# Softmax cross-entropy over a 32000-word vocabulary: label gathers spread into the load stream, narrower last chunks, results written in four parts

## Chip, cores, metric

The kernel runs on one core of one Trainium2 chip. The metric is device time in microseconds (us) of one execution. Executions agree closely (2544.47 to 2544.96 us over 12 runs of the kernel before). The TensorE does no work here.

Engine names in the profile: DVE is the vector engine, ACT the scalar engine, POOL is GpSimd, SP is the sync engine. "Lnnn" is a line of the kernel that the view belongs to, so the same statement has another number before and after the change. "half" is the tile of the first DVE instruction on a chunk, which folds the chunk in half. The start of that instruction is taken as the moment at which a chunk has landed, where DVE was waiting for it; the landing is recorded 0.02 us earlier.

## The reference

```python
batch, seq, vocab = 16, 512, 32000          # logits f32 ~ N(0,1), labels int
logits_max  = np.max(logits, axis=-1, keepdims=True)
log_sum_exp = np.log(np.sum(np.exp(logits - logits_max), axis=-1)) + logits_max.squeeze(-1)
loss = log_sum_exp - logits[b, s, labels[b, s]]        # (16, 512) f32, rewritten
```

The logits are 8192 rows of 32000 floats, 1.049 GB, each read once. The output is 32 KB.

## The kernel before

128 partitions hold 64 rows each (JT = 64). A row comes in two chunks of 16000. POOL issues each load, which converts f32 to bf16 on the way. DVE takes the maximum (folding the chunk in half, then reducing), and ACT computes exp with the sum as a by-product. The logit at the label is fetched by 64 indirect loads, each bringing one block of 16 floats per partition.

```python
    W = 16000; NCH = 2                                    # cut
    data = ctx.enter_context(tc.tile_pool(name="data", bufs=4))
    scratch = ctx.enter_context(tc.tile_pool(name="scratch", bufs=3))
    nc.gpsimd.dma_start(out=labels_sb, in_=labels_pj)
    # ... index arithmetic on DVE -> ugather
    for j in range(JT):
        nc.gpsimd.indirect_dma_start(out=B_all[:, j], out_offset=None, in_=logits_blk,
            in_offset=bass.IndirectOffsetOnAxis(ap=ugather[:, j : j + 1], axis=0))
    # ... mask16 = (k16 == label & 15) * B_all ; G = sum over 16   (all rows at once)
    for j in range(JT):
        for c in range(NCH):
            chunk = data.tile([P, W], BF16)
            nc.gpsimd.dma_start(out=chunk, in_=logits_pjv[:, j, c * W : (c + 1) * W])
            half = scratch.tile([P, W // 2], BF16)
            nc.vector.tensor_tensor(out=half, in0=chunk[:, : W // 2], in1=chunk[:, W // 2 :], op=max)
            nc.vector.tensor_reduce(out=negm[:, c : c + 1], in_=half, axis=X, op=max, negate=True)
            nc.scalar.activation(out=chunk, in_=chunk, func=Exp, bias=negm[:, c : c + 1],
                                 scale=1.0, accum_out=ssum[:, c : c + 1])
        # ... weights exp(max_c - max) join the chunks: negM_all[:, j], S_all[:, j]
    nc.scalar.activation(out=lse, in_=S_all, func=Ln)
    # ... loss = lse - negM_all - G
    nc.gpsimd.dma_start(out=out_pj, in_=loss)
```

## Time and profile before

| | us |
|---|---|
| time, median of 12 runs | 2544.6 |
| span in the profiled run | 2542.9 |
| first chunk issued / first vector instruction on it | 84.7 / 106.5 |
| pace of the load stream, per chunk of 16000 | 18.89 |
| last chunk landed | 2505.2 |
| output issued / span ends | 2534.4 / 2542.9 |

From the page of the kernel before: its busy times, two of the rows of 40 equal slices of the span (busy tenths of the DMA engines, and GB/s written), and groups of instructions (line, engine, operation, out<-in, count; busy us, mean ns of one; idle time before them and its main releaser).

```profile
span 2542.9 us, 1282 instructions
DVE 1667.2 (66%) x456; ACT 1771.0 (70%) x323; POOL 131.7 (5%) x200
DMA  0799999999999999999999999999999999999993
GB/s 7 145 213 216 218 217 217 218 217 217 217 217 217 217 217 217 217 217 217 216 215 215 216 217 217 217 218 217 218 217 217 217 217 217 217 217 217 217 217 75
...
L139 ACT ACTIVATE chunk<-chunk,negm 128x16000 bf16<-128x16000 bf16 x128 | 1744.4, 13628 | 656.0 <-issue 629.1
L132 DVE TENSOR_REDUCE negm<-half 128x1 f32<-128x8000 bf16 x128 | 1086.2, 8486 | 4.2
L126 DVE TENSOR_TENSOR half<-chunk 128x8000 bf16<-128x8000 bf16 x128 | 553.7, 4325 | 759.4 <-DMA chunk<-in_logits_dram 759.4
L84 POOL DMA_INDIRECT B_all<-in_logits_dram,ugather x64 | 61.2, 957 | 20.0 <-issue 18.9
```

No compute engine is above 70%, while the DMA row stands at 9 in every slice but the first two and the last. DVE waits 759 us for chunks and needs 12.8 us (4.33 + 8.49) per chunk, ACT 13.8; a chunk arrives every 18.89 us. The load stream is the limit. 8.192 MB of f32 in 18.89 us is 434 GB/s. The Trainium skill, "DMA: Bandwidth & Descriptors", section Bandwidth, puts the ceiling of the fabric at 435 GB/s, and what this trace reads stands at that figure. The page derives it from the SBUF ports, however, and after the conversion to bf16 only 217 GB/s are written there, so which part sets the pace is not shown. The three weak slices are what there is to win.

From the timeline of the kernel before, its head and its end (start us, duration us, engine, line, what; idle before and releaser in brackets):

```profile
4.29 1.75 POOL L84 DMA_INDIRECT B_all<-in_logits_dram,ugather  x1 [0.83 <-DVE ugather L77]
6.34 0.96 POOL L84 DMA_INDIRECT B_all<-in_logits_dram,ugather  x1 [0.30 <-issue]
...
83.77 0.94 POOL L84 DMA_INDIRECT B_all<-in_logits_dram,ugather  x1 [0.30 <-issue]
84.70 2.27 POOL L122 DMA_DIRECT2D chunk<-in_logits_dram  x4
106.48 4.32 DVE L126 TENSOR_TENSOR half<-chunk 128x8000 bf16<-128x8000 bf16 x1 [17.90 <-DMA chunk<-in_logits_dram]
...
2505.18 4.32 DVE L126 TENSOR_TENSOR half<-chunk 128x8000 bf16<-128x8000 bf16 x1 [6.04 <-DMA chunk<-in_logits_dram]
2509.54 8.49 DVE L132 TENSOR_REDUCE negm<-half 128x1 f32<-128x8000 bf16 x1
2518.11 13.63 ACT L139 ACTIVATE chunk<-chunk,negm 128x16000 bf16<-128x16000 bf16 x1 [5.16 <-issue]
2532.04 1.28 ACT L178 ACT_TABLE_LOAD   x1
2534.40 0.55 POOL L186 DMA_DIRECT2D out_dram<-loss  x1 [77.23 <-DVE loss L185]
```

Until 84.7 us POOL issues gathers, one each 1.25 us, and the first chunk is issued right behind the last of them. At the end, the last chunk still has a full chain of DVE and ACT ahead of it, 28.9 us, and after the output is issued another 8.55 us pass.

### The profile page before, as it was taken

What the parts mean: (1) busy time and instruction counts of PE and PEld (TensorE: products, weight loads), DVE (VectorE), ACT (ScalarE), POOL (GpSimd) and SP (SyncE); (2) the same over time, 40 slices, a digit from 0 to 9 for tenths busy, and PEclk for the clock granted to TensorE, in tenths of its full rate; (3) what the DMA queues carried; (4) which work ended last, traced back from release to release, by engine and by line L of the source; (5) the groups of instructions that cost most, each with busy time, mean ns of one, the idle gap of its engine ahead of it and who ended that gap; (6) DMA issues with size and microseconds to landing.
All of it is one profiled execution on the core that took longest, in us unless ns stands there. A gap on an engine that the chain in (4) does not pass through costs nothing.

```text
span 2542.9 us, 1282 instructions
## 1 busy us (share of the span) xinstructions
DVE 1667.2 (66%) x456; ACT 1771.0 (70%) x323; POOL 131.7 (5%) x200
## 2 busy tenths in 40 slices
DVE  0276676676776766767767667667677676676674
ACT  0176777767767777777677677777776776777766
POOL 7200000000000000000000000000000000000000
DMA  0799999999999999999999999999999999999993
GB/s 7 145 213 216 218 217 217 218 217 217 217 217 217 217 217 217 217 217 217 216 215 215 216 217 217 217 218 217 218 217 217 217 217 217 217 217 217 217 217 75
DMA packets 20555, 525.01 MB, mean 206 GB/s; under 512 B 3104, under 2 KB 4128, under 8 KB 4160
## 3 DMA queue, kind: packets, MB, share of 16 engines
q0 software_dynamic: 20544, 524.92, 96.0%
q14 instruction: 11, 0.09, 0.0%
HBM read 1049.17 MB, written 0.03 MB: 413 GB/s over the span
## 4 chain that ended last, share of the span: by engine, by line
issue 94%; POOL 5%; DMA 0%; POOLq 0%; DVE 0%; PEldq 0%
POOL chunk L122 3%; POOL B_all L84 2%; DMA B_all<-in_logits_dram,ugather 0%; DMA labels_sb<-in_labels_dram 0%; POOLq L122 0%; POOLq L212 0%; DVE ugather L77 0%; DVE lab_hi L52 0%; DVE lab_lo L60 0%; PEldq L212 0%; POOLq L186 0%
## 5 line engine op out<-in xcount | busy, mean ns | idle before, releaser
L139 ACT ACTIVATE chunk<-chunk,negm 128x16000 bf16<-128x16000 bf16 x128 | 1744.4, 13628 | 656.0 <-issue 629.1
L132 DVE TENSOR_REDUCE negm<-half 128x1 f32<-128x8000 bf16 x128 | 1086.2, 8486 | 4.2
L126 DVE TENSOR_TENSOR half<-chunk 128x8000 bf16<-128x8000 bf16 x128 | 553.7, 4325 | 759.4 <-DMA chunk<-in_logits_dram 759.4
L122 POOL DMA_DIRECT2D chunk<-in_logits_dram x128 | 67.7, 530 | 2304.8 <-ACT chunk L139 1149.4
L139 ACT ACT_TABLE_LOAD x1 | 1.3, 1283 | 106.5 <-DMA chunk<-in_logits_dram 106.5
L84 POOL DMA_INDIRECT B_all<-in_logits_dram,ugather x64 | 61.2, 957 | 20.0 <-issue 18.9
L102 DVE TENSOR_TENSOR mask<-mask,B_all 128x1024 f32<-128x1024 f32 x1 | 1.2, 1226 | 81.0 <-DMA B_all<-in_logits_dram,ugather 81.0
L139 ACT ACTIVATION_READ_ACCUMULATOR chunk<-chunk,negm 128x1 f32 x128 | 23.8, 186 | 0.0
L164 DVE TENSOR_TENSOR sw<-ssum,wgt 128x2 f32<-128x2 f32 x64 | 9.7, 151 | 13.6 <-ACT wgt L156 13.6
L156 ACT ACTIVATE wgt<-negm,negM_all 128x2 f32<-128x2 f32 x64 | 17.9, 279 | 0.0
L167 DVE TENSOR_REDUCE S_all<-sw 128x1 f32<-128x2 f32 x64 | 9.9, 154 | 2.0
L149 DVE TENSOR_REDUCE negM_all<-negm 128x1 f32<-128x2 f32 x64 | 9.9, 154 | 2.0
L186 POOL DMA_DIRECT2D out_dram<-loss x1 | 0.6, 552 | 77.2 <-DVE loss L185 77.2
L52 DVE TENSOR_SCALAR lab_hi<-labels_sb 128x64 int32<-128x64 int32 x1 | 0.2, 195 | 3.4 <-DMA labels_sb<-in_labels_dram 3.4
L178 ACT ACT_TABLE_LOAD x1 | 1.3, 1283 | 0.0
L106 DVE TENSOR_REDUCE G<-mask 128x64 f32<-128x1024 f32 x1 | 1.2, 1220 | 0.0
L94 DVE TENSOR_TENSOR mask<-k,lab_lo 128x1024 f32<-128x1024 int32 x1 | 1.2, 1219 | 0.0
L92 POOL IOTA k<- 128x1024 int32 x1 | 1.2, 1217 | 0.0
L182 DVE TENSOR_TENSOR loss<-lse,negM_all 128x64 f32<-128x64 f32 x1 | 0.2, 224 | 1.2 <-ACT lse L178 1.2
L45 POOL DMA_DIRECT2D labels_sb<-in_labels_dram x1 | 0.7, 707 | 0.8 <-PEq L212 0.8
L178 ACT ACTIVATE lse<-S_all 128x64 f32<-128x64 f32 x1 | 0.3, 256 | 0.0
L77 DVE CUSTOM_DVE_ANT_0 ugather<-ublock,lab_hi 128x128 uint16<-128x128 uint16 x1 | 0.2, 225 | 0.0
(7 smaller groups left out, 1.0 us busy)
## 6 DMA issues: line engine op xcount, KB each, us to landing
chunk<-in_logits_dram POOLq DMA_DIRECT2D x128, 4000.0 KB
B_all<-in_logits_dram,ugather POOLq DMA_INDIRECT x64
labels_sb<-in_labels_dram POOLq DMA_DIRECT2D x1, 64.0 KB
out_dram<-loss POOLq DMA_DIRECT2D x1, 32.0 KB
```

The costliest lines, as they stand in the source:

```text
L84: nc.gpsimd.indirect_dma_start(out=B_all[:, j], out_offset=None, in_=logits_blk, in_offset=bass.IndirectOffsetOnAxis(ap=ugather[:, j : j + ...
L92: nc.gpsimd.iota(k16, pattern=[[0, JT], [1, 16]], base=0, channel_multiplier=0)
L94: nc.vector.tensor_tensor(out=mask16, in0=k16, in1=lab_lo4.rearrange("p (j one) -> p j one", one=1).to_broadcast([P, JT, 16]), op=mybir.Al ...
L122: nc.gpsimd.dma_start(out=chunk, in_=logits_pjv[:, j, c * W : (c + 1) * W])
L126: nc.vector.tensor_tensor(out=half, in0=chunk[:, : W // 2], in1=chunk[:, W // 2 :], op=mybir.AluOpType.max,)
L132: nc.vector.tensor_reduce(out=negm[:, c : c + 1], in_=half, axis=mybir.AxisListType.X, op=mybir.AluOpType.max, negate=True,)
L139: nc.scalar.activation(out=chunk, in_=chunk, func=mybir.ActivationFunctionType.Exp, bias=negm[:, c : c + 1], scale=1.0, accum_out=ssum[:, ...
L149: nc.vector.tensor_reduce(out=negM_all[:, j : j + 1], in_=negm, axis=mybir.AxisListType.X, op=mybir.AluOpType.min,)
L156: nc.scalar.activation(out=wgt, in_=negm, func=mybir.ActivationFunctionType.Exp, bias=negM_all[:, j : j + 1], scale=-1.0,)
L164: nc.vector.tensor_tensor(out=sw, in0=ssum, in1=wgt, op=mybir.AluOpType.mult)
L167: nc.vector.tensor_reduce(out=S_all[:, j : j + 1], in_=sw, axis=mybir.AxisListType.X, op=mybir.AluOpType.add,)
L178: nc.scalar.activation(out=lse, in_=S_all, func=mybir.ActivationFunctionType.Ln, bias=0.0, scale=1.0)
```

## The change

The intent is to start the stream at once, to keep it full, and to shorten what follows it. The gathers are placed after each row's chunks; labels and outputs go through SP; the last three rows are cut into narrower chunks; a fifth data buffer is paid for, in part, with one scratch buffer of half its size; the final arithmetic is done in four groups of 16 rows.

```diff
-    data = ctx.enter_context(tc.tile_pool(name="data", bufs=4))
-    scratch = ctx.enter_context(tc.tile_pool(name="scratch", bufs=3))
+    data = ctx.enter_context(tc.tile_pool(name="data", bufs=5))
+    scratch = ctx.enter_context(tc.tile_pool(name="scratch", bufs=2))
-    nc.gpsimd.dma_start(out=labels_sb, in_=labels_pj)
+    nc.sync.dma_start(out=labels_sb, in_=labels_pj)
-    for j in range(JT):
+    def issue_gather(j):
         nc.gpsimd.indirect_dma_start(out=B_all[:, j], ...)
-    k16 = persist.tile([P, JT, 16], INT32)
+    k16 = persist.tile([P, JT, 16], INT16)
+    edges = [0, 16, 32, 48, 64]; NQ = 3                  # shortened
+    def finale(jlo, jhi):      # mask, G, Ln, loss of these rows, then:
+        nc.sync.dma_start(out=out_pj[:, sl], in_=loss[:, sl])
     for j in range(JT):
+        widths = {-3: [8000] * 4, -2: [8000] * 2 + [4000] * 4,
+                  -1: [4000] * 6 + [2000] * 4}.get(j - JT, [W] * NCH)
         # ... the loop over chunks, now over widths
+        if j < last_g:                                   # last_g = 59
+            issue_gather(j)
+        elif j == last_g:
+            for jj in range(last_g, JT): issue_gather(jj)
         # ... joining of chunks
+        if (j + 1) in edges[1:]: finale(lo, j + 1)
-    nc.scalar.activation(out=lse, in_=S_all, func=Ln)    # and the rest, once for all rows
-    nc.gpsimd.dma_start(out=out_pj, in_=loss)
```

(Cut: renamed slices, an assertion, the branch for a row in one chunk, the iota of k16 that moves behind row 3.)

More of the change, by code (lines that the diff above doesn't have):

```diff
@@ L11 @@
 INT32 = mybir.dt.int32
+INT16 = mybir.dt.int16
 @with_exitstack
@@ L31 @@
     NCH = V // W
+    NCH_MAX = 16
     logits_2d = logits.rearrange("b s v -> (b s) v")
@@ L89 @@
         )
-    k16 = persist.tile([P, JT, 16], INT32)
-    nc.gpsimd.iota(k16, pattern=[[0, JT], [1, 16]], base=0, channel_multiplier=0)
+    k16 = persist.tile([P, JT, 16], INT16)
     mask16 = persist.tile([P, JT, 16], FP32)
-    nc.vector.tensor_tensor(
-        out=mask16,
-        in0=k16,
-        in1=lab_lo4.rearrange("p (j one) -> p j one", one=1).to_broadcast(
-            [P, JT, 16]
-        ),
-        op=mybir.AluOpType.is_equal,
-    )
-    nc.vector.tensor_tensor(
-        out=mask16, in0=mask16, in1=B_all, op=mybir.AluOpType.mult
-    )
@@ L105 @@
-    G = persist.tile([P, JT], FP32)
-    nc.vector.tensor_reduce(
-        out=G,
-        in_=mask16,
-        axis=mybir.AxisListType.X,
-        op=mybir.AluOpType.add,
-    )
+    G = persist.tile([P, JT], FP32)
     negM_all = persist.tile([P, JT], FP32)
     S_all = persist.tile([P, JT], FP32)
-    for j in range(JT):
-        negm = stats.tile([P, NCH], FP32)
-        ssum = stats.tile([P, NCH], FP32)
-        for c in range(NCH):
-            chunk = data.tile([P, W], BF16)
+    lse = persist.tile([P, JT], FP32)
@@ new lines @@
+    loss = persist.tile([P, JT], FP32)
+    if JT % 16 == 0 and JT >= 32:
+        edges = list(range(0, JT, 16)) + [JT]
+    else:
+        edges = [0, JT]
+    NQ = 3
+    def finale(jlo, jhi):
+        sl = slice(jlo, jhi)
+        nc.vector.tensor_tensor(
+            out=mask16[:, sl],
+            in0=k16[:, sl],
+            in1=lab_lo4[:, sl]
+            .rearrange("p (j one) -> p j one", one=1)
+            .to_broadcast([P, jhi - jlo, 16]),
+            op=mybir.AluOpType.is_equal,
+        )
+        nc.vector.tensor_tensor(
+            out=mask16[:, sl], in0=mask16[:, sl], in1=B_all[:, sl],
+            op=mybir.AluOpType.mult,
+        )
+        nc.vector.tensor_reduce(
+            out=G[:, sl],
+            in_=mask16[:, sl],
+            axis=mybir.AxisListType.X,
+            op=mybir.AluOpType.add,
+        )
+        nc.scalar.activation(
+            out=lse[:, sl],
+            in_=S_all[:, sl],
+            func=mybir.ActivationFunctionType.Ln,
+            bias=0.0,
+            scale=1.0,
+        )
+        nc.vector.tensor_tensor(
+            out=loss[:, sl], in0=lse[:, sl], in1=negM_all[:, sl],
+            op=mybir.AluOpType.subtract,
+        )
+        nc.vector.tensor_tensor(
+            out=loss[:, sl], in0=loss[:, sl], in1=G[:, sl],
+            op=mybir.AluOpType.subtract,
+        )
+        nc.sync.dma_start(out=out_pj[:, sl], in_=loss[:, sl])
@@ new lines @@
+    for j in range(JT):
+        small = j >= JT - NQ and W % 4 == 0 and JT > NQ
+        widths = {-3: [8000] * 4, -2: [8000] * 2 + [4000] * 4, -1: [4000] * 6 + [2000] * 4}.get(j - JT, [W] * NCH) if small else [W] * NCH
+        nchj = len(widths)
+        assert sum(widths) == V
+        starts = [sum(widths[:c]) for c in range(nchj)]
+        negm = stats.tile([P, NCH_MAX], FP32)
+        ssum = stats.tile([P, NCH_MAX], FP32)
+        for c in range(nchj):
+            wj, c0 = widths[c], starts[c]
+            chunk_t = data.tile([P, W], BF16, name="chunk")
+            chunk = chunk_t[:, :wj]
@@ L122 @@
             nc.gpsimd.dma_start(
-                out=chunk, in_=logits_pjv[:, j, c * W : (c + 1) * W]
+                out=chunk, in_=logits_pjv[:, j, c0 : c0 + wj]
             )
-            half = scratch.tile([P, W // 2], BF16)
+            half_t = scratch.tile([P, W // 2], BF16, name="half")
+            half = half_t[:, : wj // 2]
             nc.vector.tensor_tensor(
                 out=half,
-                in0=chunk[:, : W // 2],
-                in1=chunk[:, W // 2 :],
+                in0=chunk[:, : wj // 2],
+                in1=chunk[:, wj // 2 :],
@@ L146 @@
             )
-        if NCH > 1:
+        if j == 3:
+            nc.gpsimd.iota(k16, pattern=[[0, JT], [1, 16]], base=0, channel_multiplier=0)
+        last_g = max(0, JT - 5)
+        if j < last_g:
+            issue_gather(j)
+        elif j == last_g:
+            for jj in range(last_g, JT):
+                issue_gather(jj)
+        if nchj > 1:
             nc.vector.tensor_reduce(
                 out=negM_all[:, j : j + 1],
-                in_=negm,
+                in_=negm[:, :nchj],
                 axis=mybir.AxisListType.X,
@@ L154 @@
             )
-            wgt = stats.tile([P, NCH], FP32)
+            wgt = stats.tile([P, NCH_MAX], FP32)
             nc.scalar.activation(
-                out=wgt,
-                in_=negm,
+                out=wgt[:, :nchj],
+                in_=negm[:, :nchj],
                 func=mybir.ActivationFunctionType.Exp,
@@ L162 @@
             )
-            sw = stats.tile([P, NCH], FP32)
+            sw = stats.tile([P, NCH_MAX], FP32)
             nc.vector.tensor_tensor(
-                out=sw, in0=ssum, in1=wgt, op=mybir.AluOpType.mult
+                out=sw[:, :nchj],
+                in0=ssum[:, :nchj],
+                in1=wgt[:, :nchj],
+                op=mybir.AluOpType.mult,
             )
@@ L168 @@
                 out=S_all[:, j : j + 1],
-                in_=sw,
+                in_=sw[:, :nchj],
                 axis=mybir.AxisListType.X,
@@ L173 @@
         else:
-            nc.vector.tensor_copy(out=negM_all[:, j : j + 1], in_=negm)
-            nc.vector.tensor_copy(out=S_all[:, j : j + 1], in_=ssum)
-    lse = persist.tile([P, JT], FP32)
-    nc.scalar.activation(
-        out=lse, in_=S_all, func=mybir.ActivationFunctionType.Ln, bias=0.0, scale=1.0
-    )
-    loss = persist.tile([P, JT], FP32)
-    nc.vector.tensor_tensor(
-        out=loss, in0=lse, in1=negM_all, op=mybir.AluOpType.subtract
-    )
-    nc.vector.tensor_tensor(out=loss, in0=loss, in1=G, op=mybir.AluOpType.subtract)
-    nc.gpsimd.dma_start(out=out_pj, in_=loss)
+            nc.vector.tensor_copy(out=negM_all[:, j : j + 1], in_=negm[:, :1])
+            nc.vector.tensor_copy(out=S_all[:, j : j + 1], in_=ssum[:, :1])
+        if (j + 1) in edges[1:]:
+            lo = edges[edges.index(j + 1) - 1]
+            finale(lo, j + 1)
 _INS = ['logits', 'labels']
```

## The prediction

> **What bounds it now.** The DMA stream of logits. The page's slices show DMA at 9 tenths and 216 to 218 GB/s (written as bf16) in every slice from the third to the last but one, while DVE has 66% and ACT 70%. The timeline shows the pace: half (DVE) starts every 18.89 us ((2505.18 - 106.48)/127), for 12.8 us of DVE work (4.33 + 8.49) and 13.8 us of ACT work (13.63 + 0.19) per chunk. The Trainium skill ("DMA: Bandwidth & Descriptors", Bandwidth) gives a fabric ceiling of 435 GB/s; 8.192 MB in 18.89 us is 434, so the trace agrees. The steady stage cannot get faster: 128 x 18.89 = 2417.5 us remain. POOL's long waits for ACT before chunk are slack: about 2.5 chunks are queued ahead (the last was issued at 2456.6 and landed at 2505.2).
>
> Outside that stream are two stretches:
> - Head: 64 gathers, 1.25 us apart on POOL (0.94 busy + 0.30), precede the first chunk issue at 84.7 us. Windows 0 to 84 us: DMA share 0.08.
> - Tail: last chunk lands 2505.18, the loss is ready at about 2534.1 (DVE 12.8, ACT 13.8, table load 1.28, small operations), output issued 2534.4, span ends 2542.9.
>
> **What the change does.**
> 1. Chunk issues no longer stand behind the gathers. First chunk issue at about 1.3 to 2 us instead of 84.7: about -83 us, all on the critical path.
> 2. The last chunk is 2000 wide instead of 16000: from landing to loss about 7 to 8 us instead of 28.9: about -21 us.
> 3. The gathers move into the saturated stream, and the DMA engines are the bottleneck, so their time is paid there. Before's gather packets (16 of 512 B per gather, one per engine) took 0.09 us on average plus about 0.02 for the semaphore packet: 64 x 0.12 = 7.7 us (estimate; up to 20 if a short packet between long ones breaks their overlap). Their 1.25 us on POOL is hidden.
> 4. The last three rows have 14 more chunks: 112 more packets per engine. A 32000 B packet took 2.375 us; at some 0.02 us fixed each this is 2 to 3 us. I expect no starving: with five buffers, my queue arithmetic from these durations shows no gap; with four there would be about 7 us. In the steady stage the fifth buffer brings nothing.
> 5. Four finales instead of one: three extra pairs of Ln/Exp table loads (1.28 each in the trace) and waits of DVE on ACT fall into ACT's 5 us and DVE's 6 us idle per chunk: free. The int16 iota is free.
>
> **Sum.** First packet 2.6 + stream 2417.5 + gathers 7.7 + small packets 2.5 + landing 1.5 + compute tail 8 + ending 8.5 = 2448 us of span; plus the 1.75 us that time exceeds span before: **2450 us** (-3.7%), range 2441 to 2462. Faster by over 2%: 0.95; within 2%: 0.04; slower: 0.01.
>
> **What would show it.** Step 1: first half starts at about 23 us, not 106. Step 2: last landing to output issue under 10 us. Step 3: pace per full chunk between rows 0 and 58 about 18.95 (one gather per two chunks); 18.89 would mean gathers are free, above 19.05 that they break the stream. Step 4: DMA share stays near 1 until the last landing. Step 5: DMA share unbroken at the finales of rows 16, 32, 48.
>
> **What would make it wrong.** Gathers costing 0.3 us or more each among large packets; gathers or finales that hold POOL or DVE longer than 2.5 chunks; the narrow end starving the DMA.

## The result and the profile after

The changed kernel took 2436.13 us (median of 8 runs, 2436.03 to 2436.24) against 2544.6. The ratio is 0.9574, with a 95% interval of 0.9564 to 0.9583. Ratios here are the mean time of one kernel's runs over that of the other's of the same rounds, so not quite the ratio of the medians quoted. The direction and the two main gains, at the head and at the tail, were as predicted; the time lies 14 us below the predicted 2450 and 5 us below the bottom of the range.

From the page of the changed kernel, the answering lines:

```profile
span 2434.2 us, 1413 instructions
DVE 1668.9 (69%) x499; ACT 1782.3 (73%) x360; POOL 205.0 (8%) x212
DMA  9999999999999999999999999999999999999998
GB/s 211 215 215 219 219 218 212 219 220 215 216 220 216 215 219 218 218 215 216 219 218 217 215 216 218 219 217 215 216 218 218 218 213 218 218 218 218 212 216 172
...
L178 ACT ACTIVATE chunk<-chunk,negm 128x16000 bf16<-128x16000 bf16 (+3 forms) x142 | 1748.2, 12311 | 556.8 <-issue 524.3
L171 DVE TENSOR_REDUCE negm<-half 128x1 f32<-128x8000 bf16 (+3 forms) x142 | 1088.2, 7663 | 3.9
L165 DVE TENSOR_TENSOR half<-chunk 128x8000 bf16<-128x8000 bf16 (+3 forms) x142 | 555.8, 3914 | 748.2 <-DMA chunk<-in_logits_dram 748.0
L87 POOL DMA_INDIRECT B_all<-in_logits_dram,ugather x64 | 126.8, 1981 | 135.1 <-DMA chunk<-in_logits_dram 104.0
```

Work is the same; the holes in the DMA row are gone. The means of the first three groups mix four widths, so they are not comparable with before's. Gathers take POOL twice as long (126.8 us against 61.2). "GPSIMD Engine Reference" of the Trainium skill, section 1 Specifications, says that POOL's SBUF interface is shared with DVE instructions that have two SBUF inputs, as half has. The trace of after agrees:

```profile
533.54 4.32 DVE L165 TENSOR_TENSOR half<-chunk 128x8000 bf16<-128x8000 bf16 x1 [5.81 <-DMA chunk<-in_logits_dram]
533.77 4.93 POOL L87 DMA_INDIRECT B_all<-in_logits_dram,ugather  x1 [12.19 <-DMA chunk<-in_logits_dram]
539.01 0.95 POOL L87 DMA_INDIRECT B_all<-in_logits_dram,ugather  x1 [0.30 <-issue]
```

The first gather, issued during half, took 4.93 us and ended 0.84 us after half did; the next, beside a reduction with one input, took 0.95. So it is throughout: the 19 gathers issued during a half took 3.8 to 4.9 us and ended 0.82 to 0.85 us after it, the other 45 took 0.94 to 1.02. No cost of its own shows for it, since POOL has time to spare (8% busy).

From the timeline of the changed kernel, head and end:

```profile
1.38 1.22 POOL L160 DMA_DIRECT2D chunk<-in_logits_dram  x2 [0.35 <-issue]
3.52 1.02 POOL L87 DMA_INDIRECT B_all<-in_logits_dram,ugather  x1 [0.92 <-DVE ugather L79]
23.40 4.32 DVE L165 TENSOR_TENSOR half<-chunk 128x8000 bf16<-128x8000 bf16 x1 [20.16 <-DMA chunk<-in_logits_dram]
...
2424.33 0.68 DVE L165 TENSOR_TENSOR half<-chunk 128x1000 bf16<-128x1000 bf16 x1 [0.48 <-DMA chunk<-in_logits_dram]
2427.74 1.94 ACT L178 ACTIVATE chunk<-chunk,negm 128x2000 bf16<-128x2000 bf16 x1
2429.99 1.28 ACT L129 ACT_TABLE_LOAD   x1
2431.94 0.33 SPq L144 DMA_DIRECT2D out_dram<-loss  x1
```

The first half starts 83.1 us earlier (23.40 against 106.48). From last landing to output issue 7.6 us pass instead of 29.2. From output issue to the end of the span it is 2.3 us instead of 8.55.

Moving before's stream to the earlier start would land the last chunk at 2505.18 - 84.70 + 1.38 = 2421.9; it landed at 2424.3. So gathers and narrow chunks together cost 2.5 us, where the prediction had 10.2 (7.7 + 2.5). With the 6.2 us of the ending that is the whole miss. Both terms were put to experiments.

The compiler's scheduler did not leave the gathers at one per row. The trace has 12 gathers up to 392 us, after the first two one for every two chunks; from 480 to 787 us there are mostly three between two chunks, and then none. The stretches of the stream can therefore be told apart.

One thing went otherwise than forecast without showing in the time. At each of the three early finales (a finale is the final arithmetic of 16 rows) ACT had Ln next in line, and stood waiting for DVE's last sum, 23 us each time. From the timeline of after and its windows (window, length, DVE, ACT and POOL busy, clock, DMA share, GB/s), at rows 0 to 15:

```profile
654.96 1.28 ACT L129 ACT_TABLE_LOAD   x1
679.28 0.22 ACT L129 ACTIVATE lse<-S_all 128x16 f32<-128x16 f32 x1 [23.03 <-DVE S_all L219]
...
660.00:680.00 20.00, 13.22 (x6) 0.70 (x2) 7.44 (x4) 1.00 1.06 228
```

The next exponential began at 680.81, some 21 us late at the pace of the stream. The DMA share is unbroken all the same: chunks had been issued far enough ahead (in the median one lands 67.4 us after its issue).

### The profile page after: what moved, and what is told of

Same layout as the page of the kernel before. It is cut to its first block, busy times and chain, and to the rows that moved or that the text cites. A ratio compares the mean times of both kernels' runs of the same rounds, so it can differ in the third digit from the quotient of the medians.

```text
span 2434.2 us, 1413 instructions
## 1 busy us (share of the span) xinstructions
DVE 1668.9 (69%) x499; ACT 1782.3 (73%) x360; POOL 205.0 (8%) x212
## 4 chain that ended last, share of the span: by engine, by line
issue 35%; DVE 31%; DMA 16%; another core or an unknown queue 15%; POOL 3%; ACT 0%; POOLq 0%; ACTq 0%; PEldq 0%
DVE negm L171 20%; DMA chunk<-in_logits_dram 16%; DVE half L165 10%; POOL B_all L87 1%; POOL chunk L160 1%; ACT chunk L178 0%; DVE negM_all L198 0%; DVE S_all L219 0%; DVE sw L213 0%; DVE mask L111 0%; ACT L129 0%; POOLq L160 0%; ACT wgt L205 0%; ACTq L257 0%
## 5 line engine op out<-in xcount | busy, mean ns | idle before, releaser
L178 ACT ACTIVATE chunk<-chunk,negm 128x16000 bf16<-128x16000 bf16 (+3 forms) x142 | 1748.2, 12311 | 556.8 <-issue 524.3
L171 DVE TENSOR_REDUCE negm<-half 128x1 f32<-128x8000 bf16 (+3 forms) x142 | 1088.2, 7663 | 3.9
L165 DVE TENSOR_TENSOR half<-chunk 128x8000 bf16<-128x8000 bf16 (+3 forms) x142 | 555.8, 3914 | 748.2 <-DMA chunk<-in_logits_dram 748.0
L160 POOL DMA_DIRECT2D chunk<-in_logits_dram x142 | 76.7, 541 | 2077.3 <-ACT chunk L178 987.6
L87 POOL DMA_INDIRECT B_all<-in_logits_dram,ugather x64 | 126.8, 1981 | 135.1 <-DMA chunk<-in_logits_dram 104.0
L178 ACT ACT_TABLE_LOAD x4 | 5.1, 1283 | 23.5 <-DMA chunk<-in_logits_dram 23.4
L205 ACT ACTIVATE wgt<-negm,negM_all 128x2 f32<-128x2 f32 (+1 forms) x64 | 17.9, 280 | 0.0
L213 DVE TENSOR_TENSOR sw<-ssum,wgt 128x2 f32<-128x2 f32 (+1 forms) x64 | 9.7, 151 | 3.6 <-ACT wgt L205 3.6
L219 DVE TENSOR_REDUCE S_all<-sw 128x1 f32<-128x2 f32 (+1 forms) x64 | 9.8, 154 | 1.7
L198 DVE TENSOR_REDUCE negM_all<-negm 128x1 f32<-128x2 f32 (+1 forms) x64 | 9.8, 153 | 1.6
L129 ACT ACT_TABLE_LOAD x4 | 5.1, 1283 | 0.1
## 6 DMA issues: line engine op xcount, KB each, us to landing
chunk<-in_logits_dram POOLq DMA_DIRECT2D x122, 4000.0 KB, 67.4
```

Source lines behind the costliest of these rows:

```text
L129: nc.scalar.activation(out=lse[:, sl], in_=S_all[:, sl], func=mybir.ActivationFunctionType.Ln, bias=0.0, scale=1.0,)
L160: nc.gpsimd.dma_start(out=chunk, in_=logits_pjv[:, j, c0 : c0 + wj])
L165: nc.vector.tensor_tensor(out=half, in0=chunk[:, : wj // 2], in1=chunk[:, wj // 2 :], op=mybir.AluOpType.max,)
L178: nc.scalar.activation(out=chunk, in_=chunk, func=mybir.ActivationFunctionType.Exp, bias=negm[:, c : c + 1], scale=1.0, accum_out=ssum[:, ...
L198: nc.vector.tensor_reduce(out=negM_all[:, j : j + 1], in_=negm[:, :nchj], axis=mybir.AxisListType.X, op=mybir.AluOpType.min,)
L205: nc.scalar.activation(out=wgt[:, :nchj], in_=negm[:, :nchj], func=mybir.ActivationFunctionType.Exp, bias=negM_all[:, j : j + 1], scale=-1.0,)
```

## The experiments

All are edits of the changed kernel, "after" below, except E1. Medians are given; each call ran the kernel before too, at 2544.59 to 2544.74.

### E1, E2, E3: why did the ending shrink by 6.2 us?

The views of the profile leave out an engine's closing instructions, but the trace records them. POOL closes with a long instruction named DRAIN, and the other engines' last instructions come only after it (in before, SP's and ACT's next ones start at 2542.38, 0.17 us after it):

```
kernel   last output issued   output landed   POOL's closing DRAIN        span ends
before   2534.40 by POOL      2536.14         2534.38 to 2542.21 (7.84)   2542.95
after    2431.94 by SP        2433.35         2417.53 to 2428.44 (10.91)  2434.24
```

The theory: the output was in place early in both, and before's ending waited for the drain. The rivals: the transfer's size and shape, or something else in the change.

**E1: the kernel before with its output on SP.**

```diff
-    nc.gpsimd.dma_start(out=out_pj, in_=loss)
+    nc.sync.dma_start(out=out_pj, in_=loss)
```

> The kernel before with only the last output transfer issued by SP instead of POOL. Question: why was the ending (output issue to end of span) 8.55 us before and 2.3 us after the change. Theory D (the closing drain of POOL): in the trace of before the output had landed at 2536.14, 1.7 us after its issue, but POOL's closing drain ran from 2534.38 for 7.84 us; it starts only when POOL has issued its last transfer. With the output on SP the drain starts after the last chunk issue (2456.6) and is hidden: time falls by about 6.2 us to about 2538.4, ending about 2.3 us. Rival S (size and shape: one output of 32 KB in rows of 256 B against 8 KB in rows of 64 B): time stays within 1 us of 2544.6. Rival F (the rest of the change, not the issuing engine, shortens the ending): also unchanged.

Measured: 2538.09 us (2538.03 to 2538.17), correct, 6.5 less than before (ratio 0.9974, 95% interval 0.9959 to 0.9990: under 2%, but clear of the noise). The ending was 2.36 us with the same 32 KB in rows of 256 B. Size and shape are out, and so is the rest of the change.

**E2: after with its last output on POOL.**

```diff
-        nc.sync.dma_start(out=out_pj[:, sl], in_=loss[:, sl])
+        q = nc.gpsimd if jhi == JT else nc.sync
+        q.dma_start(out=out_pj[:, sl], in_=loss[:, sl])
```

> The changed kernel with only the last of its four outputs issued by POOL instead of SP. Theory D: POOL's closing drain waits for this issue, the ending grows to about 8.5 us and the time to about 2442.3 (+6.2). Rival S (size): the transfer is still 8 KB in 64 B rows, so the time stays at 2436.1 within 1 us.

Measured: 2443.7 us (2443.69 to 2443.73), correct, 7.6 more than after; 1.4 above the figure expected. The output landed at 2434.01, 1.7 us after its issue, while the drain ran from 2432.28 for 8.90 us.

**E3: after, with outputs on SP and one tiny POOL copy that needs the loss.**

```diff
         nc.sync.dma_start(out=out_pj[:, sl], in_=loss[:, sl])
+        if jhi == JT:
+            late = persist.tile([P, 1], FP32)
+            nc.gpsimd.tensor_copy(out=late, in_=loss[:, JT - 1 : JT])
```

> The changed kernel with its outputs on SP, and one tiny copy of a 128x1 column on POOL that needs the final loss, issued by no transfer. It parts two forms of theory D. D1: the closing drain is a fixed time of POOL after its last instruction of any kind: +6 us, about 2442. D2: the drain's time is owed to software transfers still recent on POOL's queue (their descriptors and completions), whose last one is the chunk issued some 14 us earlier and whose clearing has run meanwhile or can run at once: under +2 us, below 2438. The drain's length in the trace is read as well (7.84 us before, 10.9 us after the change).

Measured: 2443.01 us (2442.85 to 2443.24), correct, 6.9 more than after. From the timeline of E3, its last two entries:

```profile
2432.24 0.33 SPq L144 DMA_DIRECT2D out_dram<-loss  x1
2432.28 0.18 POOL L147 COPY late<-loss 128x1 f32<-128x1 f32 x1 [13.89 <-DVE loss L140]
```

The output goes through SP as in after, POOL copies 128 numbers in 0.18 us, and the span ends at 2441.48. The drain's record is 2432.25 for 8.46 us. Form D1 holds: no POOL transfer was outstanding, and POOL still closed for some 8 us after its last instruction. What the drain does in that time no run shows. Its length was not quite fixed either (7.84, 8.90, 8.46). Where loads are still under way, the drain outlasts them: in E1 it ran from 2456.41 to 2508.55, 3.6 us past the landing of the last chunk, in after 4.1 us past it, and in E4 below, where it lasted 8.36 us, 1.5 us past it.

### E4, E5: what does a gather cost in the full stream?

**E4: after without gathers (a wrong result).**

```diff
+    nc.vector.memset(B_all, 0.0)
     def issue_gather(j):
+        return
```

> The changed kernel without its 64 gathers (the gathered tile is set to zero once, so the result is wrong on purpose: it lacks the label's logit). It measures what gathers cost in the loaded stream. The prediction said 7.7 us (0.12 each): then about 2428.4. Theory Q: queued behind full packets a gather's 512 B packet costs only its transfer, 27 ns plus 9 for the semaphore, because its memory latency is hidden; 64 x 0.035 = 2.2 us: about 2433.9. Rival Z: gathers are free, and the 0.1 us per chunk seen in rows 13 to 23 comes from POOL issuing late: then removing them gives also the 2 us, so this run parts only Q and Z together from the prediction; a second run with every gather doubled parts them.

Measured: 2434.21 us (2434.11 to 2434.3), wrong (relative error 0.09), 1.9 less than after. The last landing came 1.7 us earlier, at 2422.62.

**E5: after with every gather issued twice.**

```diff
     def issue_gather(j):
+        for dst in (B_all, B_two):                       # B_two: a tile like B_all
+            gather_into(dst, j)
+    def gather_into(dst, j):
-            out=B_all[:, j],
+            out=dst[:, j],
```

> The changed kernel with each gather issued twice, the second time into another tile that nothing reads. Removing the 64 gathers gave 1.9 us. Theory Q (64 packets of 512 B per engine, each paying its transfer of some 27 ns and its semaphore of 9, added to a full stream): another 64 cost the same again, +1.5 to +3 us, about 2438. Rival Z (the packets are free, and 2 us were lost through POOL issuing chunks late where gathers crowd): the added POOL work makes the crowding worse, and the chunk pace rises unevenly above 19.1 us where three to six gathers stand between two chunks: +4 us or more. The prediction's figure of 0.12 us each: +7.7, about 2443.8.

Measured: 2437.9 us (2437.73 to 2438.03), correct, 1.8 more than after. None, 64 and 128 gathers give 2434.2, 2436.1 and 2437.9: a straight line of 0.03 us per gather. No further loss from crowding appears (rival Z). The pace says the same. It is counted from the starts of half, with 2.5 gathers per chunk in the middle stretch of after:

| pace, us per chunk | 20 to 480 us | 480 to 830 us | 830 to 2280 us |
|---|---|---|---|
| after (gathers in it) | 18.886 (16) | 18.954 (46) | 18.887 (0) |
| E4, no gathers | 18.878 | 18.875 | 18.894 |
| E5, gathers twice | 18.910 (24) | 18.935 (42) | 18.917 (58) |

Runs with the same gathers as after (E2, E3, E11) agree with it to 0.001 us in the last two columns, but range from 18.886 to 18.907 in the first, so nothing is read from that one. In E5 the scheduler spread the gathers over all three stretches, and no stretch comes near rival Z's 19.1. The prediction had named its own test: about 18.95 us per chunk over rows 0 to 58. After has 18.902 there, and E4 18.888. That the middle column reads 18.954 is no success of the forecast: it meant one gather per two chunks, and this is 2.5 per chunk.

The packet records show why the prediction's 0.09 us per packet was too much. A gather is one 512 B packet on each of the 16 DMA engines. In before, on engines that had nothing else to do, these packets lasted 91 ns on average (median 40, longest 352). In after, queued behind full packets, the same packets lasted 33 ns on average (median 27, longest 40). That the missing part is memory latency, hidden by the queue, fits this; it is an inference.

### E6: are five buffers needed?

```diff
-    data = ctx.enter_context(tc.tile_pool(name="data", bufs=5))
+    data = ctx.enter_context(tc.tile_pool(name="data", bufs=4))
```

> The changed kernel with four data buffers instead of five. The prediction's arithmetic said that four would starve the narrow end by about 7 us, in gaps at the first narrow chunks of 8000 and 4000 and at the 2000 wide ones, and that the fifth buffer brings nothing in the steady stage: about 2443, with an unchanged pace of 18.87 to 18.9 up to row 58. Rival: the gathers in flight make the queue shallower, so that with four the steady pace suffers too (over 19.0 where three gathers stand between chunks): above 2446. Other rival: the fifth buffer is worth nothing at all: within 1 us of 2436.1.

Measured: 2441.15 us (2441.01 to 2441.2), correct, 5.0 more than after. The stretch from 830 to 2280 us keeps 18.886 us per chunk, and its last half starts at 2272.54 (after: 2272.66), so nothing is lost up to there. (The scheduler placed the gathers otherwise, 46 of them before 480 us; this stretch has none in either.) Windows over the last stretches show where it goes (window, length, DVE, ACT and POOL busy, clock, DMA share, GB/s). Those of E6:

```profile
2280.00:2380.00 100.00, 75.96 (x32) 81.74 (x22) 4.75 (x9) 1.00 0.99 209
2380.00:2388.00 8.00, 5.32 (x3) 8.00 (x5) 1.05 (x2) 1.00 0.79 148
2388.00:2423.00 35.00, 25.61 (x19) 28.66 (x18) 4.22 (x8) 1.00 1.04 213
2423.00:2431.00 8.00, 4.40 (x6) 8.00 (x7) 0.53 (x1) 1.00 0.66 119
```

And those of after, each ending with its own last landing:

```profile
2280.00:2380.00 100.00, 77.37 (x30) 83.03 (x22) 4.75 (x9) 1.00 1.00 213
2380.00:2388.00 8.00, 5.97 (x7) 8.00 (x6) 1.05 (x2) 1.00 1.04 217
2388.00:2417.00 29.00, 21.47 (x16) 25.79 (x16) 3.69 (x7) 1.00 1.03 214
2417.00:2424.00 7.00, 6.62 (x7) 5.99 (x7) 0.53 (x1) 1.00 0.78 154
```

With four buffers the DMA share falls to 0.79 soon after the widths drop from 8000 to 4000; in after it is 1.04 there. It falls again, to 0.66, in the 2000 wide chunks, where even after falls to 0.78. A little is lost earlier too, where the widths drop to 8000 (209 GB/s against 213). A buffer holds one chunk whatever its width, so narrow chunks make the queue short. The fifth buffer does its work in the narrow end alone, as the prediction said. The last chunk landed 6.5 us later (2430.88), close to the predicted 7; the time grew by 5.0 only, since from landing to output issue it took 6.2 us instead of 7.6.

### E7: what do the narrow chunks earn, and cost?

```diff
-    NQ = 3
+    NQ = 0
```

> The changed kernel with every chunk 16000 wide to the last row. Two things change: the last chunk's chain from landing to loss grows from 7.6 us to before's 28.9 (+21.3), and 112 short packets per engine become 0 extra. The prediction put the short packets at 2.5 us: then the sum is +18.8, about 2455. Theory: their fixed time is hidden by the overlap of packets and costs about 0.7 us (last landing without gathers 2422.6, against 2421.9 for before's stream moved to the earlier start): +20.6, about 2456.7. The last landing should come at 2423.6 by the theory and at 2421.8 by the prediction.

Measured: 2456.55 us (2456.49 to 2456.58), correct, 20.4 more than after. The last landing was at 2423.72, 0.6 us earlier than in after, and the output was issued 28.8 us later. So 14 more transfers, 112 more packets per DMA engine, cost about 0.6 us and not 2.5. (Profiled runs with the same stream, after, E2, E3 and E11, put the last landing at 2424.33 to 2424.70, so 0.6 to 1.0; the times give 21.2 - 20.4 = 0.8.) A packet's own record does carry a fixed part: two of 16000 B last 2 x 1199 ns, one of 32000 B 2375, so 23 ns. But records overlap: eight times 2375 is 19.0 us, more than the 18.87 us between most chunks. A sum of records overstates what is paid.

### E9: the gathers first again

```diff
+    for j in range(JT):
+        issue_gather(j)
     k16 = persist.tile([P, JT, 16], INT16)
     ...
-        if j < last_g:
-            issue_gather(j)
-        elif j == last_g:
-            for jj in range(last_g, JT):
-                issue_gather(jj)
```

> The changed kernel with all 64 gathers issued ahead of the first chunk again, as before the change; end, outputs and buffers stay changed. Step 1 of the prediction: the first vector instruction on a chunk comes at about 106 us instead of 23.4 (+83), less the 1.9 us that the gathers cost in the stream: about 2517. If labels or index arithmetic, and not the gathers' 1.25 us each on POOL, held the start before, the first chunk comes well before 106. Theory Q expects also that the same gathers' packets, now alone on the DMA engines, take some 90 ns on average again, against 33 ns in the loaded stream.

Measured: 2512.35 us (2512.08 to 2512.49), correct, 76.1 more than the control; 4.7 below the figure expected. The scheduler put the first chunk ahead of the gathers (issued at 1.38) and the other four behind them (98.23). The first half therefore starts at 23.2, not 106. The expectation of its place was wrong, but its reason was not, as the windows of E9 show:

```profile
2.00:22.00 20.00, 0.52 (x3) 0.00 (x0) 6.80 (x8) 1.00 0.99 206
22.00:99.00 77.00, 12.81 (x2) 15.00 (x3) 58.51 (x59) 1.00 0.07 7
99.00:2400.00 2301.00, 1572.43 (x439) 1664.85 (x310) 66.57 (x125) 1.00 1.01 217
```

The DMA engines stand nearly idle for 77 us until POOL is through with the gathers. Labels came through SP, so it was POOL's issuing of gathers that held the stream. This run also holds both kinds of gather packet. Those that started before 25 us, behind the first chunk, lasted 29 ns on average (112 packets), and those after it, on idle engines, 76 ns (912 packets).

### E8, E10: a better end? E11: control

In after ACT is late at the end: its last four exponentials run back to back and the last one finishes 5.3 us after the last landing.

**E8** (of the line of widths, the part that changes).

```diff
-  -1: [4000] * 6 + [2000] * 4
+  -1: [4000] * 5 + [3200, 2800, 2400, 1600, 1200, 800]
```

> An attempt at a better kernel: the last row's six chunks of 4000 and four of 2000 become five of 4000, then 3200, 2800, 2400, 1600, 1200 and 800. In the changed kernel ACT was still busy with earlier chunks when the last one landed: its four 2000 wide exponentials ran back to back from 2421.9 to 2429.6, 5.3 us after the last landing at 2424.3. With a taper in the ratio of the arrivals ACT keeps up, and from the last landing about 1 us of DVE and 1.1 us of ACT remain: 2 to 3 us less, 2433 to 2434. If completions lag by engine skew rather than by size, or the fixed times of a small chunk (0.28 + 0.19 on ACT) pile up, the gain is under 1 us.

Measured: 2435.28 us (2435.14 to 2435.39), correct, ratio to before 0.9570. That is 0.85 less than after and the best of all kernels run, but less than expected: the last exponential still ended 4.0 us after the start of the last half. DVE was late too: the last chunk had landed 0.5 us before that, at 2424.34.

**E10** (the same part).

```diff
-  -1: [4000] * 6 + [2000] * 4
+  -1: [4000] * 4 + [2000] * 7 + [1200, 800]
```

> Second attempt at a better end. The first taper gained 0.85 us only: ACT was still behind, because its exponential of a chunk starts a whole DVE time after the landing (3.4 us for 4000 wide), and its fixed 0.47 us per chunk piles up below 1600. Here the last row is four chunks of 4000, seven of 2000 (DVE 1.9 and ACT 2.1 us each, under their arrival of 2.36), then 1200 and 800, so ACT has caught up well before the end: the last exponential ends some 2.6 us after the last landing instead of 5.3 (changed kernel) or 4 (first taper). About 2433.8. If five buffers of 2000 starve the queue, landings spread and it is 2436 or more.

Measured: 2436.47 us (2435.66 to 2437.46), correct: no gain, and an unsteady one. The last landing slipped to 2427.44, 3.1 us later than in after, and the last exponential ended at 2431.15, 3.7 us behind it instead of the 2.6 expected. From the timeline of E10:

```profile
2420.21 0.68 DVE L165 TENSOR_TENSOR half<-chunk 128x1000 bf16<-128x1000 bf16 x1 [2.44 <-DMA chunk<-in_logits_dram]
...
2427.99 0.36 DVE L165 TENSOR_TENSOR half<-chunk 128x400 bf16<-128x400 bf16 x1
```

DVE waits 2.44 us for a chunk that should come every 2.36: five buffers of 2000 are too short a queue. (The last half has no wait in front: DVE came to it 0.6 us after the landing.) From 2405 us to the end of the stream the DMA share was 0.87 (to 2428), against 0.94 in after (to 2424). It looks like E6's effect again, and is the case that the expectation had named; no run with more buffers was made.

**E11: after unaltered.**

> The changed kernel unaltered, as a control on the chip of these runs: 2436.1 within 0.3 us.

Measured: 2436.22 us (2436.2 to 2436.3), correct. Where another call's run is compared with after, the 2436.13 of the result is used. E5 to E8 ran on another chip than the other experiments; before took 2544.65 us there, against 2544.59 and 2544.74, at most 0.15 apart.

## Why the prediction was right or wrong

It forecast the direction, the two main gains and 87% of the total gain (94.6 of 108.5 us), but 2436.1 lies below its range of 2441 to 2462. Its sum, term by term, against the trace of after. The gather and narrow-chunk rows are the shifts of the last landing in E4 and E7; the stream row is what remains of 2424.33.

| term (us) | predicted | measured |
|---|---|---|
| first packet | 2.6 | 2.75 |
| stream and landing | 2417.5 + 1.5 | 2419.3 |
| gathers in the stream | 7.7 | 1.7 |
| narrow packets | 2.5 | 0.6 |
| last landing to output issue | 8 | 7.6 |
| output issue to end of span | 8.5 | 2.3 |
| time beyond the span | 1.75 | 1.9 |

1. *Head, "about -83 us".* Right. The first half starts at 23.4 us (predicted: about 23). E9 puts the gathers back in front of all chunks but the first, and the hole is there again (77 us).
2. *Tail, "about -21 us".* Right: 7.6 against 29.2 us from landing to output issue. E7 shows it alone: 20.4 us net of its cost.
3. *Gathers, "64 x 0.12 = 7.7 us".* The mechanism was right, since they are paid in the stream; the size was wrong by a factor of four. Packets on idle engines were used as the price of packets in a full queue. E4 gives 1.9 us, E5 1.8 us for 64 more; the pace over rows 0 to 58 is 18.902, not 18.95.
4. *Narrow packets, "2 to 3 us".* The size was wrong: 0.6 us (E7), since records of packets overlap. That four buffers would starve the end was right (E6: last landing 6.5 us later, predicted about 7). "No gap" with five was not quite: the DMA share of after is 0.78 in its last 7 us.
5. *Four finales free.* The pace after the last gather is 18.887 us, the same as before's 18.886 there, and two of the three early finales fall into that stretch. But the reason given was wrong: the wait did not fit into "ACT's 5 us and DVE's 6 us idle per chunk"; it was 23 us at each finale, and the chunks issued ahead covered it. The outcome owes something to luck, and it was not tested by a run of its own.
6. *The unnamed step, "ending 8.5".* This failed outright, for 6.2 us of the 14. The prediction copied before's ending and overlooked that the change takes the last POOL instruction out of it. E1 to E3 show that POOL's closing drain of some 8 us filled that time, and that issuing the output from SP lets the drain run beside the last exponentials.

The step that failed is thus the sum's fixed ending (8.5 us forecast, 2.3 measured); gathers (7.7 forecast, 1.7 to 1.9 measured) and narrow packets (2.5 forecast, 0.6 to 1.0 measured) were mis-sized. All three erred to the same side. Neither the ending nor the gathers alone would have carried the time below 2441.

## What to carry to other kernels

When one queue is the limit, look for the holes at both ends of it; what is moved into the stream costs its transfer there, not the duration it had on an idle engine. Do not treat the time after the last transfer as fixed: see which engine closes last, and give the last act to an engine that closes quickly (SP here, for 6.5 us in a one-line change). Narrow the last chunks to shorten the chain behind them, but count how many bytes the buffers then keep queued.

## What the Trainium skill lacked or had wrong

- No page has POOL's closing drain. "VectorE: DVE Perf Modes", section The DRAIN you can't avoid, knows the closing and opening DRAINs as about 12 ns on every engine. POOL's lasted 7.84 us in before, 8.90 in E2, and 8.46 in E3, where POOL's last act was a copy of 0.18 us.
- "DMA: Bandwidth & Descriptors", section Issuing engines are not separate DMA queues, says that spreading issues over engines only saves sequencer time. For the transfer itself that nearly holds here (landed 1.7 us after issue from POOL, 1.4 to 1.5 from SP). But moving the output from POOL to SP saved 6.5 us in E1 by way of that drain.
- The same page, section Bandwidth, calls transfers under 64 KB descriptor-dominated, and its table, of a transfer's own busy span, has 0.68 us for 4 KB. What such a transfer adds to a full stream it does not say: here a gather of 8 KB added 0.03 us (E4, E5). The section also says that for loads the HBM side, at about 358 GB/s, binds. Its own note ties that figure to two cores streaming; one core alone read 434 GB/s here (its single-core table reaches 425).
- "ScalarE: Activation LUTs", section What ACT_TABLE_LOAD costs, gives 1283 ns and another 1380 ns of drain per switch. The load took 1283 ns here, but at the end of after Ln followed 0.01 us behind it (load from 2429.99 for 1.28, Ln at 2431.28) and the exponential before the load had just ended: the switch cost 1.3 us.
